# RWKV7 layer: the two inverse chains side by side, the second one's finish inside the scan, decays in place, parameters loaded early

## The chip, the cores and the metric

One core of a Trainium2 chip runs the whole program; the other cores are idle. The metric is the time of one execution in device microseconds (us). The engines are PE (matmuls), DVE (vector), ACT (activations and scaled copies), POOL (GpSimd) and SP, which here does nothing but issue DMAs: its queue is in order, so a DMA that waits for data holds every DMA behind it.

## The reference

Two transformer layers are run forward on 512 tokens of width 1024 in fp32. Layer 0 mixes with sparse attention, layer 1 with the recurrent mixer RWKV7; the change is in layer 1. What matters of it:

```
xx = shift(u) - u
proj = lambda i: (u + xx * mu[i]) @ w_in[:, part i]
r, k, v = proj(0), proj(1), proj(2)
w = -softplus(-(w0 + tanh(proj(3)) @ w_w2)) - 0.5
a = sigmoid(a0 + proj(4) @ w_a2)
kk = normalised(k * k_k);  k_mod = k * (1 + (a - 1) * k_a);  decay = exp(-exp(w))
def step(state, inp):                       # 512 steps, 16 heads of 64 x 64
    sa = einsum('bhvk,bhk->bhv', state, -kk_t)
    state = state * w_t + sa (x) (kk_t * a_t) + v_t (x) k_t
    return state, einsum('bhvk,bhk->bhv', state, r_t)
```

## The kernel before, in words

fp32 products are made of three matmuls of high and low parts; each weight tile is loaded by SP (`raw`), split by ACT (`whi`) and DVE (`wlo`). A tile framework decides the order of instructions on each engine from its own simulated times, except in the scan (`run`), whose order on PE, DVE, ACT and POOL is as written. SP's order is always the framework's.

The 512 steps are cut into 8 chunks of 64 tokens. In a chunk the recurrence is a triangular 64 x 64 system for each head, and the kernel inverts all 128 of these systems ahead of the scan, in two halves `th` of four chunks each. The stages of the layer, in order:

- `decay` and `gate` make the decay and gate projections; `decays` turns the summed decays `cums` into exponentials; `dense(1, ...)` makes the keys and hands each 128 x 512 tile to `key`, which builds the sides `A` and `B` of the systems. `root` and `normalise` scale them, `systems` multiplies and masks them and writes the systems to DRAM (`md`), `corners` and `blocks` read them back.
- `blocks(th)` inverts the 32 x 32 diagonal blocks by 31 steps of forward substitution on POOL, two dependent operations a step (L1038 and L1040, tiles `tmpi` and `two`). It is called "chain 0" and "chain 1" below.
- `whole(th)` calls `double(th)`, which joins the blocks to 64 x 64 inverses: a transposed copy (L1054, ACT), a trip through DRAM (`td`), two rounds of 128 small matmuls (L1074, L1076) and their evictions.
- Beside this, `dense(0, ...)` makes the receptances (`receive`, `bonus`) and `dense(2, ...)` the values, whose evictions (`value`) go by `tmp` to DRAM (`vpark`, L1112) and come back to `xh` by `fetch` (L1254).
- `run` is the scan: 19 cycles, two for each chunk, a cycle taking the chunk's inverse, products with the state and the output. `given(u)` (L1170) is the first product of a cycle; the second half's inverses are wanted from cycle 9 on.

The order as written ahead of the scan is chain 0 beside the receptances, `bonus`, half of the value matmuls, `whole(0)`, chain 1 beside the other half, the places of the scan, `whole(1)`, `run`.

Of the kernel before, what the change touches and what calls it, by code (L numbers as in the profile page):

```python
# [9 lines left out]
F32 = mybir.dt.float32  # L10
# [6 lines left out]
P = 128  # L17
S = 512
# [51 lines left out]
class Net:  # L70
    def __init__(self, ctx, tc, io):
        self.tc, self.nc, self.io = tc, tc.nc, io
        nc = self.nc
        self.const = ctx.enter_context(tc.tile_pool(name="const", bufs=1))
        self.act = ctx.enter_context(tc.tile_pool(name="act", bufs=1))
        self.ps = ctx.enter_context(tc.tile_pool(name="ps", bufs=4, space=PSUM))
        dram = ctx.enter_context(tc.tile_pool(name="park", bufs=1, space=bass.MemoryType.DRAM))
        self.hpark = dram.tile([S, D], F32, name="hpark")
        self.dram = dram
        self.ident = self.const.tile([P, P], F32, name="ident")  # L80
        self.mhalf = self.const.tile([P, 16], F32, name="mhalf")
# [12 lines left out]

# [330 lines left out]
    def nsa(self, xh, xl):  # L425
        nc, io = self.nc, self.io
        opair = self.open_pairs()
# [340 lines left out]
    def rwkv(self, u, layer):  # L768
# [11 lines left out]
        two = lambda: vp.tile([P, D], F32, tag="two", name="two", bufs=2)  # L780
# [6 lines left out]
        prm = vp.tile([P, 19 * KT], F32, name="prm")  # L787
        nc.sync.dma_start(out=prm[:, 0:12 * KT], in_=io["rwkv_prm"])
        mu = lambda i, kt: prm[:, i * KT + kt:i * KT + kt + 1]
        omu = lambda i, kt: mu(13 + i, kt)  # L790
        par = lambda i, j: prm[:, (6 + i) * KT + j:(6 + i) * KT + j + 1]
        W0, A0, KK, KA, RK, GB, OKA = range(7)
        for d, s, n in ((6 + OKA, 6 + KA, 1), (13, 0, 6)):
            nc.vector.tensor_scalar(prm[:, d * KT:(d + n) * KT], prm[:, s * KT:(s + n) * KT], -1.0, 1.0,
                                    op0=OP.mult, op1=OP.add)
# [4 lines left out]
        ind = vp.tile([P, KT, 32], F32, name="ind")  # L800
        nc.sync.dma_start(out=ind.rearrange("p k h -> p (k h)"), in_=self.cst("ind"))
        sel = vp.tile([64, CH], F32R, name="sel")
# [97 lines left out]
        def decays():  # L900
# [57 lines left out]
        def key(g, n, acc):  # L958

            j = 4 * g + n  # L960
            A, B = sides(j)
            if n == 0:
                n2[g] = self.bank("bon")
            sq, kk = tmp(), v3(tmp())
            nc.scalar.activation(sq, acc, AF.Square, scale=par(KK, j))
            nc.scalar.activation(kk, v3(acc), AF.Copy, scale=par(KK, j))
            nc.vector.tensor_mul(B[:, :, C:], B[:, :, C:], v3(acc))
            nc.tensor.matmul(n2[g][0:32, :], ind[:, j, :], sq, start=n == 0, stop=n == 3)
# [25 lines left out]
        rinv = [vp.tile([64, S], F32R, name="rinv", bufs=2) for _ in range(2)]  # L994
# [48 lines left out]
        def whole(th):  # L1043

            with ExitStack() as ctx:
                for i in anchor.values():
                    ctx.enter_context(self.tc.issue_after(i.ins))
                double(th)

        def double(th):  # L1050
# [14 lines left out]
            z = iv()  # L1065
            for w in range(2):
                for h, mt in enumerate(inv[th]):
# [9 lines left out]
                    for e in range(2):  # L1077
# [3 lines left out]
                        else:  # L1081
                            nc.scalar.activation(mt[r1, :, 32:64], zv[r1], AF.Copy, scale=-1.0)

# [4 lines left out]
        def bonus():  # L1088

            bon = self.bank("bon")  # L1090
            for j in range(KT):
# [3 lines left out]
                for b in range(NB):  # L1095
                    nc.tensor.matmul(bon[:, 16 * b + 2 * j:16 * b + 2 * j + 2], pr[:, b * P:b * P + P],
                                     ind[:, j, 2 * j:2 * j + 2], start=True, stop=True)
# [233 lines left out]
        weave(blocks(0), dense(0, 13, receive, vec))  # L1331
# [5 lines left out]
        weave(blocks(1), fill)  # L1337
# [8 lines left out]
        whole(1)  # L1346
# [76 lines left out]
def _consts():  # L1423
# [17 lines left out]
    parts["ind"] = ind.reshape(P, KT * 32)  # L1441
# [143 lines left out]
```

## Time and profile before

| | us |
|---|---|
| time, median of 3 runs | 2342.32 (2335.94, 2342.32, 2344.95) |
| the profiled execution: its time | 2344.54 |
| the profiled execution: its span | 2342.6 |
| PE busy | 2188.7 (93%) |
| POOL busy | 391.2 (17%) |

The span is the stretch from the first to the last recorded instruction; 1.9 us lie around it. The clock that PE was granted is 0.953 of full speed in the mean. Positions below are us from the span's start; layer 1's mixer stands between 1500 and 1930.

### The profile page before, as it was taken

The numbers are of one execution on the slowest core, as the hardware profiler recorded it, in microseconds if no ns is written. First come the engines' busy times: TensorE is split into PE (matmuls) and PEld (weight loads), VectorE is DVE, ScalarE is ACT, GpSimd is POOL, SyncE is SP. The second block draws the span as 40 slices with busy tenths as digits, with TensorE's granted clock in tenths as the row PEclk, the third lists the DMA queues.
The fourth block names the chain that finished last, engine by engine and source line by source line (L and its number), as shares of the span: only waits on it lengthen the run. The fifth ranks groups of instructions, "written<-read, shape, count | busy, mean of one in ns | idle before, by whom it ended". The sixth has DMA issues, their size and how long they took to land.

```text
span 2342.6 us, 38478 instructions
## 1 busy us (share of the span) xinstructions
PE 2188.7 (93%) x15398; PEld 1924.1 (82%) x15398; DVE 1531.3 (65%) x2446; ACT 1157.8 (49%) x2274; POOL 391.2 (17%) x397
## 2 busy tenths in 40 slices
PE   7999999999999899999999999796794988899998
PEld 7999888877656799998899998674684877899987
DVE  8888526356686888863688872486741546988733
ACT  5555415465574555553455562483332654555532
POOL 4000004031110400000310000125536433200000
PEclk9999999999899999999999999897887989999999
DMA  4333333211002233334223333223353023333332
GB/s 172 106 102 100 108 98 102 72 55 37 28 1 87 84 105 103 100 107 128 80 75 102 104 109 99 88 81 89 72 128 107 25 72 129 124 101 108 100 100 71
DMA packets 93284, 214.44 MB, mean 92 GB/s; under 512 B 40624, under 2 KB 41392, under 8 KB 93104
## 3 DMA queue, kind: packets, MB, share of 16 engines
q1 hardware_dynamic: 93104, 211.97, 29.2%
q8 instruction: 121, 1.98, 0.4%
q14 instruction: 59, 0.48, 0.1%
HBM read 196.94 MB, written 15.01 MB: 90 GB/s over the span
## 4 chain that ended last, share of the span: by engine, by line
issue 28%; PE 23%; POOL 7%; DVE 6%; ACT 2%; DMA 1%; SPq 0%; POOLq 0%; DVEq 0%; ACTq 0%
PE p L182 17%; POOL two L1040 2%; POOL tmpi L1038 2%; PE p L1146 1%; ACT junk L205 1%; POOL sp L334 1%; DVE h L248 1%; DVE slot L188 1%; DVE xl L188 0%; PE p L1191 0%; POOL rstd L209 0%; PE p L854 0%; POOL ab L915 0%; PE p L1170 0%; PE p L1162 0%
## 5 line engine op out<-in xcount | busy, mean ns | idle before, releaser
L182 PE MATMUL p<-xh,whi 128*128 128x256 f32 (+1 forms) x1640 | 479.0, 296 | 18.4 <-ACT xh L187 8.4
L182 PE MATMUL p<-xl,whi 128*128 128x256 f32 (+1 forms) x1640 | 476.9, 294 | 3.5 <-DVE xl L188 3.5
L182 PE MATMUL p<-xh,wlo 128*128 128x256 f32 (+1 forms) x1640 | 457.2, 294 | 1.5 <-DVE wlo L188 1.4
L182 PE MATMUL p<-whi,slot 128*128 128x512 f32 x1280 | 394.8, 389 | 0.0
L161 DVE TENSOR_TENSOR wlo<-raw,whi 128x1024 fp32r<-128x1024 f32 x150 | 189.9, 1268 | 313.4 <-ACT whi L157 313.3
L182 PE MATMUL p<-slot,whi 128*128 128x256 f32 x1920 | 362.1, 285 | 11.2 <-issue 6.0
L182 PEld LDWEIGHTS p<-xh,whi 128*128 128x128 f32 x1640 | 319.0, 195 | 29.6 <-ACT xh L187 9.8
L157 ACT ACTIVATE whi<-raw 128x1024 fp32r<-128x1024 f32 x166 | 174.7, 1057 | 336.8 <-PE p L182 321.0
L182 PEld LDWEIGHTS p<-xl,whi 128*128 128x128 f32 x1640 | 319.6, 195 | 9.0 <-DVE xl L188 4.9
L182 PEld LDWEIGHTS p<-slot,whi 128*128 128x128 f32 x1920 | 304.1, 193 | 13.6 <-issue 6.2
L182 PEld LDWEIGHTS p<-xh,wlo 128*128 128x128 f32 x1640 | 308.8, 195 | 7.1 <-DVE wlo L188 1.6
L187 ACT ACTIVATE whi<-xn 128x1024 fp32r<-128x1024 f32 (+1 forms) x240 | 220.0, 917 | 185.0 <-PE p L182 136.9
L188 DVE TENSOR_TENSOR wlo<-xn,whi 128x1024 fp32r<-128x1024 f32 (+1 forms) x240 | 255.3, 1065 | 50.8 <-ACT whi L187 47.6
L182 PEld LDWEIGHTS p<-whi,slot 128*128 128x128 f32 x1280 | 240.0, 188 | 49.7
L182 PE MATMUL p<-slot,wlo 128*128 128x256 f32 x960 | 270.8, 284 | 0.0
L209 POOL TENSOR_TENSOR rstd<-rstd,mhalf 128x1 f32<-128x1 f32 x48 | 30.0, 627 | 1348.5 <-DVE rstd L208 1347.6
L182 PE MATMUL p<-wlo,slot 128*128 128x512 f32 x640 | 249.0, 389 | 0.0
L182 PEld LDWEIGHTS p<-slot,wlo 128*128 128x128 f32 x960 | 185.1, 193 | 0.0
L378 ACT ACTIVATE sp<-p 128x256 f32<-128x256 f32 x320 | 121.0, 378 | 112.9 <-PE p L182 112.8
L182 PEld LDWEIGHTS p<-wlo,slot 128*128 128x128 f32 x640 | 120.1, 188 | 24.9
L188 DVE TENSOR_TENSOR wlo<-raw,whi 128x1024 fp32r<-128x1024 f32 x80 | 97.7, 1221 | 10.0 <-ACT whi L187 9.9
L187 ACT ACTIVATE whi<-raw 128x1024 fp32r<-128x1024 f32 x80 | 84.1, 1051 | 39.2 <-PE p L182 39.2
(322 smaller groups left out, 3781.6 us busy)
## 6 DMA issues: line engine op xcount, KB each, us to landing
raw<-in_wpack SPq DMA_DIRECT2D x252, 512.0 KB, 3.6
xn<-in_wpack SPq DMA_DIRECT2D x80, 512.0 KB, 3.5
hpark<-h SPq DMA_DIRECT2D x8, 512.0 KB, 2.6
h<-hpark SPq DMA_DIRECT2D x8, 512.0 KB, 4.8
h<-in_x SPq DMA_DIRECT2D x4, 512.0 KB, 7.2
gpost<-in_ffn_norm_post SPq DMA_DIRECT2D x4, 512.0 KB, 6.6
md<-tb SPq DMA_DIRECT2D x8, 256.0 KB, 3.0
td<-two SPq DMA_DIRECT2D x4, 512.0 KB, 3.0
```

What stands on the lines that cost most here:

```text
L157: self.last_hi = nc.scalar.activation(hi, raw, AF.Copy)
L161: (eng or nc.vector).tensor_sub(lo, raw, hi.bitcast(F32))
L182: m = self.nc.tensor.matmul(out, lhs[a], rhs[b], start=start and i == 0, stop=stop and i == 2, skip_group_check=more)
L187: i = self.nc.scalar.activation(hi, src, AF.Copy)
L188: return i, (eng or self.nc.vector).tensor_sub(lo, src, hi.bitcast(F32))
L205: nc.scalar.activation(self.junk(), src[q], AF.Square, scale=1.0 / (half * math.sqrt(D)), accum_out=ss[:, q:q + 1])
L209: nc.gpsimd.tensor_tensor(r[:, 1:2], r[:, 0:1], self.mhalf[:, 0:1], op=OP.pow)
L248: nc.vector.scalar_tensor_tensor(h, t[:, sl[q]], r, h, op0=OP.mult, op1=OP.add)
L334: nc.gpsimd.tensor_sub(t4, q(xh, 1, 0, b), t2)
L378: copy = lambda dst, bank: nc.scalar.activation(dst, bank[:, 0:H], AF.Copy)
L1038: nc.gpsimd.tensor_tensor(t, ms[:, j, j + 1:32].rearrange("p (i o) -> p i o", o=1).to_broadcast([P, n, m]), T[:, j:j + 1, 0:m].to_broadcas ...
L1040: nc.gpsimd.tensor_tensor(T[:, j + 1:32, 0:m], T[:, j + 1:32, 0:m], t, op=OP.subtract)
```

## The change

- **Parameters.** `prm`, the layer's mixing, decay and key parameters, was loaded and completed (L788 to L794) at the start of layer 1. Now it lies in the pool that lives all the time and `load_prm` does this at the start of layer 0.
- **Decays in place.** For each of 8 tiles, `decays` made exp into `tmp`, exp into `A`, two POOL products (L915, L917), a DVE operation and a POOL copy. Now ACT makes the second exp in place in `cums`, and an affine copy into `A`; the two POOL products are gone.
- **Keys.** `key` made two 128 x 512 ACT operations, two DVE products, a POOL product and a POOL copy (L969, L970). Now it has one large and one 128 x 8 ACT operation, three DVE operations and one POOL product (on DVE for the last tile).
- **Buffers.** `two` has four buffers, not two; `rinv` one for each, not two; `sel` lies in a `two`, `ind` is a 128 x 64 table.
- **Chains.** `blocks(1)` comes right after `blocks(0)`; chain 1 no longer runs beside the value matmuls after `whole(0)`.
- **Second inverse.** `double` is split into `convert` (transposed copy and the trip through DRAM) and two halves of matmuls. `convert(1)` is issued after cycle 5 of the scan, the halves of `double(1)` after cycles 7 and 8. Nothing of them stands ahead of the scan.

```diff
@@ -424,6 +437,7 @@
     def nsa(self, xh, xl):
         nc, io = self.nc, self.io
+        self.load_prm()
...
-        two = lambda: vp.tile([P, D], F32, tag="two", name="two", bufs=2)
+        two = lambda: vp.tile([P, D], F32, tag="two", name="two", bufs=4)
...
-                cum, aa = v3(cums[j]), B[:, :, C:]
-                em = v3(tmp())
-                nc.scalar.activation(em, cum, AF.Exp, scale=kap[:, 0:1])
-                nc.scalar.activation(A[:, :, C:], cum, AF.Exp, scale=kap[:, 1:2])
-                nc.gpsimd.tensor_mul(A[:, :, 0:C], aa, em)
-                nc.vector.tensor_scalar(aa, aa, par(KA, j), par(OKA, j), op0=OP.mult, op1=OP.add)
-                nc.gpsimd.tensor_mul(aa, aa, em)
+                nc.scalar.activation(A[:, :, C:], v3(cums[j]), AF.Exp, scale=kap[:, 1:2])
+                nc.scalar.activation(cums[j], cums[j], AF.Exp, scale=kap[:, 0:1])
+                nc.scalar.activation(A[:, :, 0:C], B[:, :, C:], AF.Identity, scale=par(KA, j), bias=par(OKA, j))
                 nc.gpsimd.tensor_copy(pc[:, j, :], A[:, :, 2 * C - 1])
...
-            sq, kk = tmp(), v3(tmp())
-            nc.scalar.activation(sq, acc, AF.Square, scale=par(KK, j))
-            nc.scalar.activation(kk, v3(acc), AF.Copy, scale=par(KK, j))
-            nc.vector.tensor_mul(B[:, :, C:], B[:, :, C:], v3(acc))
...
-            nc.gpsimd.tensor_mul(B[:, :, 0:C], kk, A[:, :, 0:C])
-            nc.gpsimd.tensor_copy(A[:, :, 0:1], kk[:, :, 0:1])
-            nc.vector.tensor_mul(A[:, :, 1:C], kk[:, :, 1:], A[:, :, C:2 * C - 1])
...
+            nc.scalar.activation(sq, acc, AF.Square, scale=kk)
+            nc.vector.tensor_mul(en, k, v3(cums[j]))
...
+            nc.vector.scalar_tensor_tensor(B[:, :, 0:C], en, kk, B[:, :, C:], op0=OP.mult, op1=OP.mult)
+            (nc.vector if j == KT - 1 else nc.gpsimd).tensor_mul(B[:, :, C:], en, A[:, :, 0:C])
+            nc.scalar.activation(A[:, :, 0:1], k[:, :, 0:1], AF.Copy, scale=kk)
+            nc.vector.scalar_tensor_tensor(A[:, :, 1:C], k[:, :, 1:], kk, A[:, :, C:2 * C - 1], op0=OP.mult, op1=OP.mult)
...
+                weave(double(th, *convert(th)))
+
+        def convert(th):
...
                 for u in range(-1, NU + 3):
                     cycle(u, X, s1, bvs, gw)
+
+                    if u == 5:
+                        dbl = double(1, *convert(1))
+                    if u >= 7:
+                        next(dbl, None)
...
-        weave(blocks(0), dense(0, 13, receive, vec))
+        weave(blocks(0))
+        weave(blocks(1))
+        weave(dense(0, 13, receive, vec))
...
         whole(0)
-        weave(blocks(1), fill)
         weave(fill)
...
         self.kinds["iv"] = (2, 3)
-        whole(1)
         run(X, *places)
```

How the order of instructions moves is seen at three places. On POOL at the end of chain 0 there stood, before, the clearing of the scan's `xh`, then the clearing of chain 1's tile and chain 1's first step:

```order
L1038 TENSOR_TENSOR tmpi<-two 128x31
L1040 TENSOR_TENSOR two<-two,tmpi 128x31
L1127 MEMSET xh 64x3072
L1032 MEMSET two 128x1024
L1033 MEMSET two 128x32
L1038 TENSOR_TENSOR tmpi<-two 128x31
L1040 TENSOR_TENSOR two<-two,tmpi 128x31
```

After the change POOL goes at the same place from the last step of chain 0 into the first steps of chain 1:

```order
L1043 TENSOR_TENSOR tmpi<-two 128x31
L1045 TENSOR_TENSOR two<-two,tmpi 128x31
L1043 TENSOR_TENSOR tmpi<-two 128x31
L1045 TENSOR_TENSOR two<-two,tmpi 128x31
L1043 TENSOR_TENSOR tmpi<-two 128x60
L1045 TENSOR_TENSOR two<-two,tmpi 128x30x2
```

The clearing of chain 1's tile has moved into chain 0, that of `xh` into chain 1, and the six L1237 products for the scan, which stood inside chain 1, behind it.

On SP, the queue ahead of the scan was before the weights, the value writes (`vpark`) with the fetches (`xh`), the reading of chain 1's systems, four weights and the other value writes:

```order
L143 DMA raw<-in_wpack 128x1024 x3
L1112 DMA vpark<-tmp 128x512 x3
L1254 DMA xh<-vpark 64x512
L1112 DMA vpark<-tmp 128x512
L1254 DMA xh<-vpark 64x512
L1030 DMA two<-md_15225 64x32x32 x2
L1254 DMA xh<-vpark 64x512
L143 DMA raw<-in_wpack 128x1024 x4
L1112 DMA vpark<-tmp 128x512 x3
```

After the change, chain 1's systems are read long before, and the writing of chain 1's result (`td_17737`) stands in this queue ahead of the value writes:

```order
L156 DMA raw<-in_wpack 128x1024 x3
L1060 DMA td_17737<-two 128x1024
L1120 DMA vpark<-tmp 128x512 x4
L1262 DMA xh<-vpark 64x512 x3
L156 DMA raw<-in_wpack 128x1024 x4
L1120 DMA vpark<-tmp 128x512 x3
```

The framework has drawn that one write of `convert(1)` ahead of the scan; the rest of it is issued in the scan. All rows behind it now wait for the end of chain 1.

On PE, before, the second inverse's matmuls stood between the first two `given` products of the scan:

```order
L1170 MATMUL p_17199<-xh,big 64x64 x7
L1074 MATMUL p_17264<-two,xl 32x32
L1074 MATMUL p_17299<-two,xl 32x32
L1074 MATMUL p_17264<-two,xl 32x32 x31
L1074 MATMUL p_17299<-two,xl 32x32 x31
L1076 MATMUL p_17334<-xl,two 32x32 x32
L1076 MATMUL p_17369<-xl,two 32x32 x32
L1162 MATMUL p_17416<-ident,ab 128x128 x4
```

After the change the next cycle's transposes follow there at once, and the first round of these matmuls is found behind cycle 7 of the scan:

```order
L1154 MATMUL p_17933<-ab 128x128
L1081 MATMUL p_17949<-two,xl 32x32 x32
L1081 MATMUL p_17984<-two,xl 32x32 x32
L1190 MATMUL p_17177<-xh,xl 64x64 x8
L1199 MATMUL p_17175<-xh,ab 64x64 x8
```

The second round stands in the same way behind cycle 8. Elsewhere, half of the decay matmuls and the gate weights' splits move ahead of the last input transposes.

## Rows read from the trace of the kernel before

**Rows 1.** Windows of 10 us at the scan's start and inside the scan.

```profile
core 0: us, PE busy (x) PEld busy (x) DVE busy (x) ACT busy (x) POOL busy (x), PEclk, DMA share, GB/s
1790.00:1800.00 10.00, 0.00 (x0) 0.00 (x0) 0.00 (x0) 0.00 (x0) 8.69 (x17) 0.50 0.00 0
...
1850.00:1860.00 10.00, 9.75 (x230) 8.61 (x228) 6.67 (x19) 6.78 (x32) 5.71 (x9) 1.00 0.10 30
```

**Rows 2.** Timeline of PE: start, length, line, and idle time before with its releaser.

```profile
1519.74 6.71 PE L854 MATMUL p<-xh,whi 128*128 128x256 f32 x16 [4.91 <-DVE whi L849]
...
1593.70 1.54 PE L968 MATMUL p<-tmp,ind 128*32 128x512 f32 x2 [1.98 <-ACT tmp L965]
...
1754.50 2.21 PE L1076 MATMUL p<-xl,two 32*32 32x32 f32 x128
...
1779.81 0.68 PE L1170 MATMUL p<-xh,big 128*64 128x64 f32 x14
1808.63 0.39 PE L1074 MATMUL p<-two,xl 32*32 32x32 f32 x4 [28.14 <-issue]
...
1820.28 0.33 PE L1170 MATMUL p<-xh,big 128*64 128x64 f32 x2 [0.78 <-DVE big L1153]
```

**Rows 3.** Timeline of POOL, chain 0 and chain 1.

```profile
1663.16 0.24 POOL L1038 TENSOR_TENSOR tmpi<-two 128x31 f32<-128x31 f32 x1 [21.08 <-DMA two<-md]
...
1719.81 0.25 POOL L1040 TENSOR_TENSOR two<-two,tmpi 128x31 f32<-128x31 f32 x1
1720.00 2.66 POOL L1127 MEMSET xh<- 64x3072 f32 x1
1756.84 0.95 POOL L1032 MEMSET two<- 128x1024 f32 x1 [34.18 <-PE p L1076]
...
1802.16 0.25 POOL L1040 TENSOR_TENSOR two<-two,tmpi 128x31 f32<-128x31 f32 x1
```

**Rows 4.** Timeline of ACT.

```profile
1517.62 1.33 ACT L829 ACTIVATE tb<-xh,prm 128x512 f32<-128x512 f32 x2 [3.01 <-DVE prm L794]
...
1592.96 0.69 ACT L965 ACTIVATE tmp<-p,prm 128x512 f32<-128x512 f32 x1 [4.62 <-POOL ab L917]
...
1612.14 1.28 ACT L977 ACT_TABLE_LOAD   x1 [0.18 <-PE p L968]
...
1802.44 1.94 ACT L1054 ACTIVATE two<-two 128x1024 f32<-128x1024 f32 x1 [25.20 <-POOL two L1040]
...
1829.02 0.77 ACT L1185 ACTIVATE xh<-p 64x256 f32<-64x256 f32 x2 [0.30 <-PE p L1182]
```

**Rows 5.** Windows by stage (columns as in rows 1).

```profile
1517.00:1566.00 49.00, 44.20 (x176) 32.72 (x177) 43.49 (x58) 40.92 (x62) 1.37 (x1) 0.91 0.31 94
1566.00:1593.00 27.00, 25.72 (x114) 20.97 (x112) 15.95 (x20) 15.33 (x23) 23.58 (x27) 1.00 0.33 110
...
1663.00:1720.00 57.00, 54.15 (x235) 45.25 (x236) 50.09 (x53) 28.25 (x39) 52.06 (x62) 0.89 0.18 54
1720.00:1764.00 44.00, 43.24 (x428) 36.56 (x427) 10.99 (x18) 14.70 (x18) 8.78 (x16) 0.92 0.75 183
1758.00:1803.00 45.00, 21.71 (x127) 17.96 (x125) 9.37 (x10) 7.22 (x10) 39.10 (x69) 0.76 0.30 94
```

**Rows 6.** Lines of ACT, 1517 to 1593: busy and mean of one, idle before.

```profile
L157 ACT ACTIVATE whi<-raw 128x1024 fp32r<-128x1024 f32 x12 | 12.4, 1051 | 4.1 <-DMA raw<-in_wpack 4.0
```

**Rows 7.** Lines of POOL, 1758 to 1803.

```profile
L1237 POOL TENSOR_TENSOR tmp<-xh,bonx 64x256 f32<-64x256 f32 x6 | 3.7, 612 | 0.4
```

**Rows 8.** Lines of DVE beside chain 0, 1663 to 1720.

```profile
L830 DVE SCALAR_TENSOR_TENSOR tb<-xh,prm,tb 128x511 f32<-128x511 f32 x16 | 15.6, 999 | 4.9 <-ACT tb L829 4.8
L832 DVE TENSOR_TENSOR big<-tb,big 128x512 fp32r<-128x512 f32 x15 | 14.7, 1000 | 0.0
```

**Rows 9.** Timeline of SP's queue ahead of the scan.

```profile
1772.61 1.68 SPq L1112 DMA_DIRECT2D vpark<-tmp  x3
1777.08 1.89 SPq L1254 DMA_DIRECT2D xh<-vpark  x3
```

**Rows 10.** The page's DMA issues: KB each, us from issue to landing.

```profile
raw<-in_wpack SPq DMA_DIRECT2D x252, 512.0 KB, 3.6
```

More of the change, by code (lines that the diff above doesn't have):

```diff
@@ L83, in __init__ @@
         self.wpool = ctx.enter_context(tc.tile_pool(name="wpool", bufs=1))
+        self.prm = self.const.tile([P, 19 * KT], F32, name="prm")
         self.chunk = 0
@@ L93, in cst, with prm_parts, load_prm @@
         return self.io["consts"][0:rows, c0:c0 + n]
+    def prm_parts(self):
+        mu = lambda i, kt: self.prm[:, i * KT + kt:i * KT + kt + 1]
+        return mu, lambda i, kt: mu(13 + i, kt), lambda i, j: mu(6 + i, j)
+    def load_prm(self):
+        self.nc.sync.dma_start(out=self.prm[:, 0:12 * KT], in_=self.io["rwkv_prm"])
+        for d, s, n in ((12, 9, 1), (13, 0, 6)):
+            self.nc.vector.tensor_scalar(self.prm[:, d * KT:(d + n) * KT], self.prm[:, s * KT:(s + n) * KT], -1.0, 1.0,
+                                         op0=OP.mult, op1=OP.add)
     def push(self, name, **kw):
@@ L785, in rwkv @@
         self.junk = lambda: vp.tile([P, 512], F32, tag="tb", name="junk", bufs=2)
[L787 to L791, printed above, removed]
+        prm, (mu, omu, par) = self.prm, self.prm_parts()
         W0, A0, KK, KA, RK, GB, OKA = range(7)
-        for d, s, n in ((6 + OKA, 6 + KA, 1), (13, 0, 6)):
-            nc.vector.tensor_scalar(prm[:, d * KT:(d + n) * KT], prm[:, s * KT:(s + n) * KT], -1.0, 1.0,
-                                    op0=OP.mult, op1=OP.add)
         own = [slice(0, 64), slice(64, 128)]
@@ L799, in rwkv @@
         nc.sync.dma_start(out=tri, in_=self.cst("tri"))
-        ind = vp.tile([P, KT, 32], F32, name="ind")
-        nc.sync.dma_start(out=ind.rearrange("p k h -> p (k h)"), in_=self.cst("ind"))
-        sel = vp.tile([64, CH], F32R, name="sel")
+        ind = vp.tile([P, 64], F32, name="ind")
+        nc.sync.dma_start(out=ind, in_=self.cst("ind"))
+        sel = two().bitcast(F32R)[0:64]
         st = big()
@@ L963, in key @@
                 n2[g] = self.bank("bon")
-            sq, kk = tmp(), v3(tmp())
-            nc.scalar.activation(sq, acc, AF.Square, scale=par(KK, j))
-            nc.scalar.activation(kk, v3(acc), AF.Copy, scale=par(KK, j))
-            nc.vector.tensor_mul(B[:, :, C:], B[:, :, C:], v3(acc))
-            nc.tensor.matmul(n2[g][0:32, :], ind[:, j, :], sq, start=n == 0, stop=n == 3)
-            nc.gpsimd.tensor_mul(B[:, :, 0:C], kk, A[:, :, 0:C])
-            nc.gpsimd.tensor_copy(A[:, :, 0:1], kk[:, :, 0:1])
-            nc.vector.tensor_mul(A[:, :, 1:C], kk[:, :, 1:], A[:, :, C:2 * C - 1])
+            k, kk = v3(acc), par(KK, j)
+            sq, en = tmp(), v3(tmp())
+            nc.scalar.activation(sq, acc, AF.Square, scale=kk)
+            nc.vector.tensor_mul(en, k, v3(cums[j]))
+            nc.tensor.matmul(n2[g][0:32, :], ind[:, 30 - 2 * j:62 - 2 * j], sq, start=n == 0, stop=n == 3)
+            nc.vector.scalar_tensor_tensor(B[:, :, 0:C], en, kk, B[:, :, C:], op0=OP.mult, op1=OP.mult)
+            (nc.vector if j == KT - 1 else nc.gpsimd).tensor_mul(B[:, :, C:], en, A[:, :, 0:C])
+            nc.scalar.activation(A[:, :, 0:1], k[:, :, 0:1], AF.Copy, scale=kk)
+            nc.vector.scalar_tensor_tensor(A[:, :, 1:C], k[:, :, 1:], kk, A[:, :, C:2 * C - 1], op0=OP.mult, op1=OP.mult)
         def root(g, ts=slice(0, S)):
@@ L993, in rwkv @@
         md = [self.dram.tile([32, 2, C, C], F32, name=f"md{th}") for th in range(2)]
-        rinv = [vp.tile([64, S], F32R, name="rinv", bufs=2) for _ in range(2)]
+        rinv = [vp.tile([64, S], F32R, name="rinv", bufs=1) for _ in range(2)]
         def systems(g, th):
@@ L1064, in double @@
                         nc.sync.dma_start(out=mt[r0:r0 + 32, :, 32 * k:32 * k + 32], in_=tv[0, k, e, :, hq[h], :])
-            z = iv()
+            return t11, iv()
+        def double(th, t11, z):
             for w in range(2):
@@ L1082, in double @@
                             nc.scalar.activation(mt[r1, :, 32:64], zv[r1], AF.Copy, scale=-1.0)
+                yield
         def receive(g, n, acc):
@@ L1096, in bonus @@
                     nc.tensor.matmul(bon[:, 16 * b + 2 * j:16 * b + 2 * j + 2], pr[:, b * P:b * P + P],
-                                     ind[:, j, 2 * j:2 * j + 2], start=True, stop=True)
+                                     ind[:, 30:32], start=True, stop=True)
                 yield
@@ L1440, in _consts @@
     ind = (h == 2 * p + (i // 64)[:, :, None]).astype(f)
-    parts["ind"] = ind.reshape(P, KT * 32)
+    parts["ind"] = (np.arange(64)[None, :] == 30 + i // 64).astype(f)
     sel = np.zeros((P, KT, P), f)
```

2 lines of the change are left out of this document (removed).

## The prediction

> **What bounds the kernel now.** I read the 10 us windows around the scan's start first. From 1790 to 1800 PE, DVE and ACT do nothing at all and only POOL works; inside the scan PE is busy 9.75 of 10 us [rows 1]. So the scan is bound by PE, and ahead of it stands a hole in which everything waits for POOL. PE's timeline shows its edges: the first `given` ends at 1780.5, the second inverse's matmuls start at 1808.6, the second `given` comes at 1820.3 [rows 2]. POOL's timeline says why: chain 0 runs from 1663.2 to 1720.0, then POOL stands idle for 34 us until the first inverse's matmuls have given a buffer free, and chain 1 runs from 1757.8 to 1802.4 [rows 3]. ACT's transposed copy follows at once after 25 us of waiting [rows 4]. That is the path: keys, systems, chain 0, (idle,) chain 1, join, scan. Chain 0's own start waits for `md`, so what lies upstream of it counts too: there ACT waits 4.6 us for POOL's `ab` products before the first key eviction at 1592.96 [rows 4], and POOL is busy 23.6 of 27 us [rows 5].
>
> **A. Upstream of chain 0: about 13 us.** What holds the first key eviction? PE's first matmul with its key tile follows at 1593.70 after 1.98 us without work, so PE had done all it could by 1591.7 [rows 2]. 48 matmuls of the second key group stand between the first group's end and that point; at 25.72 us for 114 matmuls [rows 5] these are 10.9 us, so the first group was ready at 1580.8, and the eviction was late by ACT and POOL. After the change, POOL's 16 products are gone and ACT has a row of its own work. ACT was busy 40.92 + 15.33 = 56.3 us between 1517 and 1593 [rows 5]. Three weight splits of 1.05 us go ahead of that stretch [rows 6], eight affine copies come in at the 0.69 us of the 128 x 512 eviction [rows 4]: 56.3 - 3.2 + 5.5 = 58.6. I add 5 us of stalls (it had 19.7, of them 4.6 for POOL's product and 3.0 for `prm` [rows 4]) and start at 1516.8: 1580.4, which is 12.6 earlier. PE can follow: it drops 13 of its 32 first decay matmuls and the 4.9 us wait for `whi` [rows 2]. From this eviction to `root` were 19.2 us [rows 4]; the waits for `tmp` shorten it by about 2, DVE's third operation per tile gives back 1 to 2. I take 13 in all. Bounds: 4 if PE's clock falls in the gaps that it then gets, as it did to 0.50 where it starved [rows 1], or DVE becomes the limit; 20 if the stalls vanish and the second group gains as well.
>
> **B. The hole: about 30 us.** I count in the frame in which chain 0 still starts at 1663.2. Chain 0 is 56.9 us long, chain 1 44.6 with six L1237 products of 3.7 us and their gaps of 0.4 [rows 3, 7], so 40.4 by itself. Why is chain 0 longer for the same 62 operations? It runs beside 50.1 us of DVE work, chain 1 beside 9.4; POOL is busy 52.1 and 39.1 - 3.7 = 35.4 us [rows 5]. The slope is (52.1 - 35.4) / (50.1 - 9.4) = 0.41 us for each us of DVE. Chain 1 moves next to the stretch from 1720 to 1764, where DVE is busy 11.0 [rows 5]: 40.4 + 0.7 = 41.1. Its clearing (0.95, with a small one 1.1) and that of `xh` (2.7) [rows 3] now lie inside the chains. The end: 1663.2 + 56.9 + 1.1 + 41.1 + 2.7 = 1765.0.
>
> This is ahead of the first `given` (1779.8 to 1780.5), and the scan no longer waits for the second inverse there. Without that wait the second `given` follows the first by 1.1 us of transposes, 2.1 of products and 0.8 of mask: 1784.4 and not 1820.3 [rows 2], so 35.9 us go. But the write of chain 1's result now stands in SP's queue ahead of the value writes, and SP passes it only at 1765.0. Behind it: this write and four value writes at 1.68/3 = 0.56, 2.8; three fetches, 1.9 [rows 9]; a weight, 0.5 to issue and 3.6 to land [rows 10]; its split on ACT, 1.05 [rows 6], which stands ahead of the second value group's evictions; then the first eviction, 0.7. That is 1775.6, and the first write of that group at about 1776.5 to 1777, as DVE's evictions have a split ahead of them as well, where it was 1772.6 [rows 9]: 4.5 late. It costs between nothing (if the path is elsewhere) and 15 (if the evictions wait for three more weights at 3.6 each). PE then starves for some us at the lower clock: 1. So 35.9 - 4.5 - 1 = 30.4.
>
> **C. What the scan takes on: about 7 us.** The two halves of the second `double` now stand in PE's order: 2.21 us each [rows 2], and a little for ACT's evictions ahead of the next cycle's, 2.4 and 2.5. The transposed copy, 1.94 [rows 4], stands in ACT's order, where PE's product and ACT's next operation are 0.30 us apart [rows 4]: 1.7. Small waits add 0.4. The sum is 7.0; it could be 4.7 (the matmuls alone, if ACT has the room), or 17 if cycle 9 also has to wait for the trip through DRAM, which before lay in the 6.2 us between 1802.4 and 1808.6 [rows 2, 4].
>
> **D. Parameters at the start: nothing.** One load and two tiny DVE operations move to the program's start, behind the first loads of the input; no row here shows that place. If nothing covers them they cost SP 0.56 for the issue [rows 9] and DVE less than twice the 0.69 of a 128 x 512 operation, 2 us together; if DVE still waits for the input there, nothing. They are nearer to that, having 8 and 48 elements a partition against 512. Their other effect, ACT's 3.0 us wait, is in A.
>
> **The sum** against the profiled execution: 13 + 30.4 - 7 = 36.4, so 2344.5 - 36.4 = 2308.1. The median of the runs shown is 2.2 us below the profiled execution: 2306.
>
> **A rule on POOL and DVE.** The rows say that DVE's work lengthens chain 0 by 0.41 us for each us [rows 5]. Of DVE's 50.1 us there, 30.3 are operations with two inputs in SBUF, L830 and L832 [rows 8]. [...]
>
> **The rivals.**
> 1. *Chain 1 slow beside other work* (0.12). If it takes chain 0's 56.9 us instead of 41.1, its end is 1780.8, SP is held 15.8 longer: 2306 + 16 = 2322. For it: it moves next to work of PE, ACT and DMA. Against: that work is PE's, DVE is nearly idle there [rows 5].
> 2. *The hold is not felt and upstream gives 20* (0.10): 4.5 + 1 + 7 more, with 2 more from C: 2306 - 14.5 = 2291. For it: 19.7 us of ACT idle; against: PE is busy 69.9 of 76 us there [rows 5].
> 3. *Upstream gives nothing* (0.12). The freed POOL is not what decides, DVE's third operation or PE's half clock takes it: A falls to 0 to 4, 2306 + 11 = 2317.
> 4. *The second inverse is late in the scan* (0.07): cycle 9 waits up to 10 us, 2316. For it: the trip was 6.2 us and more. Against: from cycle 5 to cycle 7 there are two full cycles for it.
> 5. *The write at SP decides* (0.03), the slower side: chain 1's end holds the value path, and so the whole start of the scan, which before it did not. The gains are gone when SP is held until about 1765 + 36 = 1801, and it is slower by 0.5% from 1813: chain 1 would have to take 89 us, 2354 and more. The longest chain seen took 56.9.
>
> **How the numbers follow.** The likeliest case has 0.56, its own range being 2296 to 2316 by the bounds of A and B. The range 2286 to 2327 takes in rivals 1 to 4 at their price and leaves out two of them together and rival 5. A measurement tells about 0.5% from no change: 2330.6 and 2354 are the borders. All of the main case and rival 2, and most of 1, 3 and 4 lie below: faster 0.90; pairs of rivals reach no change: 0.07; slower 0.03.
>
> **What would show it.** Right: POOL's idle row of 34 us is gone, chain 1's first step follows chain 0's last at once and takes about 41 us; chain 0 starts near 1650; the windows without PE are gone, the second `given` comes 3 to 5 us after the first; the first key eviction is near 1580; two cycles of the scan are longer by 2.4 us, one by 1.7, and no PE wait at cycle 9. Wrong: chain 0 starts within 4 us of 1663, or chain 1 takes over 50 us, or SP's write of `td` ends a wait that reaches the scan's first products by more than 10 us.

## The result and the profile after

The changed kernel takes 2304.68 us (median of 4 runs, 2298.61 to 2306.79), the kernel before 2343.64 beside it: a ratio of 0.9833, 95% interval 0.98 to 0.9866. It is 39 us faster by the medians and 38.1 by the two profiled executions (2344.54 and 2306.49, the latter with a span of 2304.6); forecast were 36.4, and a median of 2306.

POOL's timeline after the change answers to [rows 3]:

```profile
1647.88 0.24 POOL L1043 TENSOR_TENSOR tmpi<-two 128x31 f32<-128x31 f32 x1 [22.45 <-DMA two<-md]
...
1704.42 0.25 POOL L1045 TENSOR_TENSOR two<-two,tmpi 128x31 f32<-128x31 f32 x1
1704.75 0.24 POOL L1043 TENSOR_TENSOR tmpi<-two 128x31 f32<-128x31 f32 x1
...
1720.55 2.66 POOL L1135 MEMSET xh<- 64x3072 f32 x1
...
1748.77 0.25 POOL L1045 TENSOR_TENSOR two<-two,tmpi 128x31 f32<-128x31 f32 x1
```

The idle row of 34 us is gone. Chain 0 starts at 1647.9 and chain 1's first step follows chain 0's last at once; chain 0 takes 56.8 us, chain 1 44.3 with the 2.7 of clearing `xh`, so 41.6 by itself. PE's timeline answers to [rows 2] (L1178 is `given`, L1154 `products`, L1081 and L1083 are the second inverse's matmuls):

```profile
1762.46 1.71 PE L1154 MATMUL p<-ab 64*128 64x128 f32 x16 [2.22 <-DVE tmp L1117]
...
1769.20 1.11 PE L1178 MATMUL p<-xh,big 128*64 128x64 f32 x14
...
1774.15 1.71 PE L1178 MATMUL p<-xh,big 128*64 128x64 f32 x16 [0.78 <-DVE big L1161]
...
1815.91 2.21 PE L1081 MATMUL p<-two,xl 32*32 32x32 f32 x128
...
1823.95 2.21 PE L1083 MATMUL p<-xl,two 32*32 32x32 f32 x128
```

Between the first `given` and the second there are 4 us, where there were 40, and the second inverse's matmuls stand in the scan. But PE still waits 2.22 us for DVE's eviction ahead of 1762.46, and runs slower for a while: the 16 matmuls of the second `given` take 1.71 us, where 14 took 0.68 in [rows 2]. The 10 us windows show it (columns as in [rows 1], the granted clock third from the end):

```profile
1750.00:1760.00 10.00, 10.00 (x47) 8.03 (x45) 0.95 (x1) 0.51 (x1) 0.00 (x0) 1.00 0.91 320
1760.00:1770.00 10.00, 7.78 (x55) 6.58 (x52) 6.14 (x8) 3.69 (x6) 1.23 (x2) 0.73 0.67 208
1770.00:1780.00 10.00, 8.32 (x76) 6.69 (x74) 2.58 (x4) 2.13 (x5) 2.45 (x4) 0.59 0.35 99
1780.00:1790.00 10.00, 9.59 (x222) 8.53 (x224) 4.38 (x11) 5.82 (x25) 2.27 (x3) 1.00 0.10 29
```

The clock is 0.73 and 0.59 of full speed between 1760 and 1780, behind the gap. SP's queue tells why there is a gap; it answers to [rows 9]:

```profile
1749.06 0.33 SPq L1060 DMA_DIRECT2D td<-two  x1
1749.47 2.57 SPq L1120 DMA_DIRECT2D vpark<-tmp  x4
1752.46 1.75 SPq L1262 DMA_DIRECT2D xh<-vpark  x3
1754.31 7.85 SPq L156 DMA_DIRECT2D raw<-in_wpack  x4
1762.26 1.40 SPq L1120 DMA_DIRECT2D vpark<-tmp  x3
```

The write of chain 1's result leaves when chain 1 ends, and the value writes, the fetches, four weights and the second group's value writes follow it one behind the other. This stretch, in which SP's queue stands behind that write, is called the hold. ACT's rows show how it reaches PE: the split of a weight waits 9.79 us for its load, and the second value group's evictions stand behind the split, though the matmuls that they wait for end at 1759.8:

```profile
1759.49 1.06 ACT L170 ACTIVATE whi<-raw 128x1024 fp32r<-128x1024 f32 x1 [9.79 <-DMA raw<-in_wpack]
1760.57 1.08 ACT L1119 ACTIVATE tmp<-p 128x512 f32<-128x512 f32 x2
```

ACT's timeline answers to the first key eviction in [rows 4] (1592.96 there, behind 4.62 us of waiting that are gone):

```profile
1578.01 0.67 ACT L970 ACTIVATE tmp<-p,prm 128x512 f32<-128x512 f32 x1
```

**By stages.** The stretch ahead of the mixer, where no edit touches more than the parameters' load, differs by up to 13 us from one profile to the next (below). So all profiles are read from the mixer's first transposes of the input (the first matmul with `ident` and `xn` behind 1490 us; 1500.88 in the kernel before, 1499.75 after). Each figure in the table is the start of that row, for "ends" its end, less that zero; the last column is the span less it.

| kernel | first key eviction | chain 0 starts | chain 1 ends | value matmuls end | second `given` | scan, first to last inverse product | end |
|---|---|---|---|---|---|---|---|
| before | 92.1 | 162.3 | 301.5 | 273.1 | 319.4 | 76.6 | 841.7 |
| changed | 78.3 | 148.1 | 249.3 | 260.1 | 274.4 | 83.8 | 804.9 |
| e1, chains alone | 84.5 | 152.9 | 254.9 | 264.8 | 284.3 | 83.5 | 815.0 |
| e2, upstream alone | 78.5 | 148.8 | 288.3 | 260.4 | 307.6 | 76.2 | 829.7 |
| e3, write behind fetches | 78.6 | 149.5 | 250.5 | 261.3 | 269.9 | 83.1 | 798.2 |
| e4, load called late | 78.6 | 149.0 | 250.2 | 261.1 | 275.9 | 83.2 | 805.5 |
| e5, joined before scan | 78.5 | 148.9 | 249.0 | 273.6 | 286.4 | 76.0 | 805.3 |
| e6, half of chain 1 | 78.5 | 148.8 | 229.7 | 260.7 | 269.3 | 83.2 | 797.9 |
| e7, tile's pool alone | 84.5 | 152.7 | 292.6 | 264.6 | 310.2 | 76.4 | 832.1 |
| e8, tile in layer's pool | 84.5 | 155.6 | 258.5 | 266.9 | 285.1 | 85.2 | 812.8 |
| c1, changed again | 78.5 | 149.1 | 250.2 | 261.0 | 275.9 | 83.3 | 804.8 |
| c2, e3 again | 78.5 | 149.0 | 249.9 | 260.7 | 269.3 | 83.5 | 797.9 |
| e9, join eased | 78.4 | 149.4 | 249.7 | 273.9 | 282.5 | 80.5 | 808.2 |
| e10, one input | 78.5 | 149.6 | 246.2 | 261.9 | 271.6 | 84.1 | 801.8 |

One order of instructions, profiled three times (changed, c1, e4), has 804.9, 804.8 and 805.5 in the last column, and differs by up to 1.5 us in between. So a difference of 2 us in the last column is readable, where single runs of one kernel spread by 8 to 13.

### The profile page after: what moved, and what is told of

It is laid out like the page before. It is cut to its first block, busy times and chain, and to the rows that moved or that the text cites. A ratio compares the mean times of both kernels' runs of the same rounds, so it can differ in the third digit from the quotient of the medians.

```text
span 2304.6 us, 38449 instructions
## 1 busy us (share of the span) xinstructions
PE 2190.6 (95%) x15398; PEld 1921.0 (83%) x15398; DVE 1527.2 (66%) x2447; ACT 1159.3 (50%) x2282; POOL 363.9 (16%) x372
## 4 chain that ended last, share of the span: by engine, by line
issue 29%; PE 24%; DVE 5%; POOL 4%; ACT 3%; DMA 1%; SPq 0%; DVEq 0%; POOLq 0%; ACTq 0%
PE p L195 19%; POOL two L1045 1%; POOL tmpi L1043 1%; PE p L1154 1%; ACT junk L218 1%; POOL sp L347 1%; PE p L1178 0%; DVE slot L201 0%; PE p L1170 0%; DVE xl L201 0%; DVE h L261 0%; PE p L972 0%; PE p L862 0%; PE p L1206 0%; PE p L1199 0%
## 5 line engine op out<-in xcount | busy, mean ns | idle before, releaser
L174 DVE TENSOR_TENSOR wlo<-raw,whi 128x1024 fp32r<-128x1024 f32 x150 | 190.2, 1269 | 316.7 <-ACT whi L170 316.7
L195 PEld LDWEIGHTS p<-slot,whi 128*128 128x128 f32 x1920 | 303.4, 193 | 14.9 <-issue 6.2
L195 PE MATMUL p<-wlo,slot 128*128 128x512 f32 x640 | 249.0, 389 | 0.0
L195 PE MATMUL p<-big,whi 128*128 128x512 f32 (+1 forms) x288 | 94.9, 412 | 12.0 <-ACT big L839 11.2
L200 ACT ACTIVATE whi<-raw 128x1024 fp32r<-128x1024 f32 x80 | 84.1, 1051 | 40.1 <-PE p L195 40.1
```

Of the source, the lines that this page charges most:

```text
L174: (eng or nc.vector).tensor_sub(lo, raw, hi.bitcast(F32))
L195: m = self.nc.tensor.matmul(out, lhs[a], rhs[b], start=start and i == 0, stop=stop and i == 2, skip_group_check=more)
L200: i = self.nc.scalar.activation(hi, src, AF.Copy)
```

## The experiments

**The parts taken apart (e1, e2).** e1 has the new chains with decays, keys and the call that loads the parameters as they were; e2 is the reverse.

```diff
 e1
-        self.load_prm()                        # at the start of layer 0
+        self.load_prm()                        # at the start of layer 1
-  (the new bodies of decays and key)
+  (the bodies of before)
 e2
-        weave(blocks(0))
-        weave(blocks(1))
-        weave(dense(0, 13, receive, vec))
+        weave(blocks(0), dense(0, 13, receive, vec))
...
         whole(0)
+        weave(blocks(1), fill)
         weave(fill)
...
+        whole(1)
         run(X, *places)
```

> The changed kernel with decays and key made as before and the parameters loaded at the start of layer 1; only the chains, the second inverse in the scan and the buffers are changed. Theory (the terms add up): chain 0 starts again near 1663 us, the second given comes about 31 us earlier than in the kernel before, the scan is 7 longer: 24 us faster than before, about 2320. Rival (the moved chains are the whole gain): about 2305, with chain 0 starting near 1648. Rival (without the earlier start the moved chains give nothing): about 2343.

Measured: 2312.01 us, ratio 0.9875 (0.9849 to 0.99).

> The changed kernel with the chains, the second inverse, the two-buffer tile and sel as before; decays, keys and the early parameters stay. Theory: chain 0 starts near 1648 us, everything behind it keeps its old distances, hole included: 15 us faster than before, about 2328. Rival (the earlier start is lost in the waits behind it): 2343.

Measured: 2334.1 us, ratio 0.9967 (0.9951 to 0.9982).

Neither came out as expected. e1 gained 29 us and not 24, and its table row says where: its first key eviction and chain 0 come 7.6 and 9.4 us earlier than before although its decays and keys are the old ones. Something upstream was still in it. e2 gained 7 by the median and 12 by the table: chain 0 is 13.5 earlier, as forecast, but the second `given` only 11.8. PE's row between the two rounds of the second inverse shows a wait for SP's read that the kernel before does not have:

```profile
1802.54 3.62 PE L1083 MATMUL p<-xl,two 32*32 32x32 f32 x126 [1.29 <-DMA xl<-td]
```

The clock has dropped in the hole, as before (0.64 from 1760 to 1800), but now the second `given` itself and the products behind it run at the lower level (0.50 from 1800 to 1810, 0.74 from 1810 to 1820, by e2's windows; in the kernel before it was back at 1.00 from 1820, with the second `given`). The two gains, 36 by the medians, come near to that of the change, but this proves nothing: the next runs show that one part is counted in both.

**What of the parameters it was (e4, e7, e8).** e4 moves only the call `load_prm` back to the start of layer 1.

```diff
 e4
-        self.load_prm()                        # in nsa, layer 0
+        self.load_prm()                        # ahead of prm_parts, layer 1
 e7, on the kernel before
+        self.prm = self.const.tile([P, 19 * KT], F32, name="prm")   # beside ident and mhalf
-        prm = vp.tile([P, 19 * KT], F32, name="prm")
+        prm = self.prm
 e8, on the changed kernel
-        self.prm = self.const.tile([P, 19 * KT], F32, name="prm")
+        self.prm = vp.tile([P, 19 * KT], F32, name="prm")           # and load_prm behind it
```

> The changed kernel with one thing undone: the parameters are loaded at the start of layer 1. Theory: they are the smaller part of what lies upstream of chain 0, the 3 us wait on ACT and the 3 weight splits of 1.05 us behind it: about 6 us slower than the changed kernel, 2311, chain 0 near 1654. Rival (ACT's own row of work decides, the parameters do nothing): 2305. Rival (the parameters are all of it, the decays and keys nothing): 2320, chain 0 near 1662.

Measured: 2308.85 us, ratio 0.9856 (0.9828 to 0.9883); chain 0 at 149.0 in the table. Every engine has the same instructions in the same order as in the changed kernel: the call's place in the program does nothing. SP issues the load at 6.75 us in e4 and at 6.87 in the changed kernel: the framework draws it to the program's start either way, where its tile is free. So e4 undid nothing, and e1 had the early parameters too. The place that counts is the tile's pool:

> The kernel before with one thing changed: the parameters' tile lies in the pool that lives all the time; all else, the chains too, is as before. Theory of the prediction (ACT's and POOL's work on decays and keys holds the first key eviction, the parameters are worth 3 to 6 us): 2338 to 2341. Rival, from the first four runs (the layer's pool holds the load back and with it the decay matmuls; this is most of the earlier start): chain 0 starts 9 us earlier against the mixer's first transposes, and the time is 9 us less, 2334.

Measured: 2329.02 us, ratio 0.9953 (0.9932 to 0.9973); 9.6 us less in the table.

> The changed kernel with the parameters' tile back in the layer's own pool. Theory of the prediction: 3 to 6 us slower than the changed kernel, chain 0 about 151 to 154 us after the mixer's first transposes. Rival (the tile's place is most of the earlier start): 9 us slower, 2314, chain 0 about 157 us after them.

Measured: 2307.63 us, ratio 0.9858 (0.9834 to 0.9882); 7.9 us more than the changed kernel in the table.

By the table both come near to the rival (9 us in each), and the prediction's price of 3 to 6 is too low. The medians say less: e7 is 12.6 us faster than the kernel before, but e8 only 3.0 slower than the changed kernel's first runs, which would fit the price; its profile reaches the mixer at 1493.03, 6.7 us ahead of the changed kernel's. Its chain 0 starts at 155.6, between the 151 to 154 of the theory and the rival's 157. The mechanism stands in the rows of e8: SP's load, DVE's completion and first use of the parameters, and PE's first decay matmuls:

```profile
1507.49 0.33 SPq L101 DMA_DIRECT2D prm<-in_rwkv_prm  x1
```

```profile
1509.54 0.26 DVE L104 TENSOR_SCALAR prm<-prm 128x8 f32<-128x8 f32 x2 [1.38 <-DMA prm<-in_rwkv_prm]
...
1510.92 1.89 DVE L857 TENSOR_TENSOR whi<-raw,prm 128x512 f32<-128x512 f32 x3
```

```profile
1512.36 5.24 PE L862 MATMUL p<-xh,whi 128*128 128x256 f32 x16 [4.93 <-DVE whi L857]
```

The tile in the layer's pool is not there before the layer begins, and the load is issued at 1507.5, 14 us behind the mixer's first transposes; the two completions and the weights' products follow, and PE waits 4.93 us for them. In e7, with the tile in the other pool and all else as before, the same matmuls start 5.3 us after those transposes and not 19:

```profile
1497.33 5.41 PE L855 MATMUL p<-xh,whi 128*128 128x256 f32 x16 [2.41 <-ACT xh L764]
```

**What SP's queue holds back (e3, c1, c2, e6).** e3 puts the one write of chain 1's result behind the first six fetches; e6 leaves out the last 15 of chain 1's 31 steps, so that the second half's inverses are not complete.

```diff
 e3
-            nc.sync.dma_start(out=td[1], in_=T.rearrange("p i k -> p (i k)"))
+            with ExitStack() as ctx:
+                if th:
+                    ctx.enter_context(self.tc.issue_after(fetched[NX - 1].ins))
+                nc.sync.dma_start(out=td[1], in_=T.rearrange("p i k -> p (i k)"))
 e6
-            for j in range(31):
+            for j in range(31 - 15 * th):
```

> The changed kernel with the write of chain 1's result (the one DMA that stands ahead of the value writes) put behind the first six fetches in SP's queue. Theory as in the prediction (the hold costs 4.5 us and a stretch at the lower clock): the value writes of the second group go about 4.5 us earlier after the value matmuls, the first given comes 2 to 3 us after their end and not 7; 4 to 6 us faster than the changed kernel. Rival (PE ends the value matmuls 10.8 us after chain 1's end anyway, and only the last evictions are held): 1 to 2 us. Rival (nothing of it is felt): 0.

Measured: 2292.86 us, ratio 0.9797 (0.9776 to 0.9818).

> The changed kernel with the last 15 of chain 1's 31 steps left out, so chain 1 ends some 15 to 20 us earlier; the second half's inverses are not complete. It asks what the chains still bound. Rival (the POOL chain is still the path, as it was before): 12 us faster or more than the changed kernel. Theory (PE with its value matmuls has taken over, chain 1 is felt by SP's queue alone): the value matmuls end where they did, the time falls by what the hold costs, 1 to 6 us.

Measured: 2292.8 us, ratio 0.9801 (0.9777 to 0.9825).

The two are the same, though chain 1 ends at 250.5 in e3 and 229.7 in e6. So POOL's chain is no longer the path; only the write that waits for it is. (The 12 us of e6 alone would have fitted its rival; beside e3's 12 they do not.) But that both gain 12 us by the medians is twice what was expected, and the table gives 7. To tell, the changed kernel and e3 ran again beside each other:

> The changed kernel itself once more, beside the others of this call, since the stretch ahead of the mixer (which no edit touches) differed by up to 13 us between profiles. Every theory: within 0.3% of 2305 as against the kernel before; from the mixer's first transposes to the end of the span 805 us, as in its first profile.

Measured: 2309.15 us, ratio 0.9867 (0.9843 to 0.9892).

> The changed kernel with the write of chain 1's result behind the first six fetches, once more. Theory (the hold costs what the stages show, 6 us): 6 us faster than the changed kernel of this call, and 798 to 799 us from the mixer's first transposes to the end. Rival (the 12 us between the medians of two calls are all its own): 12 us faster than the changed kernel of this call.

Measured: 2298.53 us, ratio 0.9812 (0.9785 to 0.9839); the table has 6.9.

Of the hold, 6.7 and 6.9 us are shown stage by stage in two pairs of profiles (804.9 and 804.8 against 798.2 and 797.9). Between the medians of c1 and c2 lie 10.6, nearer to the rival's 12. What the medians add can hardly be the edit's: in e3 and c2 every engine has the changed kernel's instructions in the changed kernel's order, but for nine places in SP's queue from 1749 us on. It is as large as the spread ahead of the mixer, where no place differs; that it comes from there is not shown run by run. c1's PE rows show where the 6.9 lie; its value matmuls end at 1753.15:

```profile
1768.00 0.33 PE L1178 MATMUL p<-xh,big 128*64 128x64 f32 x2 [0.78 <-DVE big L1161]
1768.60 0.68 PE L1178 MATMUL p<-xh,big 128*64 128x64 f32 x14 [0.27 <-DVE big L1161]
...
1770.88 0.68 PE L1190 MATMUL p<-xh,xl 64*64 64x64 f32 x16
```

From there to the second `given` are 14.9 us, in c2 8.6 (1757.42 to 1765.99). In c2 the same weight is split on ACT, without a wait for its load, 5.6 us before the value matmuls end, and the evictions follow the matmuls at once:

```profile
1751.86 1.06 ACT L170 ACTIVATE whi<-raw 128x1024 fp32r<-128x1024 f32 x1 [4.54 <-PE p L195]
```

It is by this that e3 is the best complete version of the study, at 0.98 of the kernel before.

**The second inverse's place (e5, e9).** e5 finishes it ahead of the scan, as before, with the chains back to back. e9 has e3's write, and issues the rest of `convert(1)` ahead of the scan, with half of the scan's evictions on DVE.

```diff
 e5
-                    if u == 5:
-                        dbl = double(1, *convert(1))
-                    if u >= 7:
-                        next(dbl, None)
...
+        whole(1)
         run(X, *places)
 e9, on e3
-                    if u == 5:
-                        dbl = double(1, *convert(1))
+            dbl = double(1, *convert(1))       # ahead of the scan
...
-                            nc.scalar.activation(z[r2, hq[h], :], zv[r2], AF.Copy)
+                            if th and e:
+                                nc.vector.tensor_copy(z[r2, hq[h], :], zv[r2])
+                            else:
+                                nc.scalar.activation(z[r2, hq[h], :], zv[r2], AF.Copy)
```

> The changed kernel with the second inverse finished ahead of the scan; the chains stay back to back. Theory (back to back is what empties the hole; the place of the second inverse is worth little): the scan loses its 7 us, the start of the scan takes on 4 to 7 us of matmuls at the lower clock and about 6 us of reads in SP's queue ahead of the value writes: about 4 us slower than the changed kernel, 2308. Rival (the move into the scan is what brings it): the scan's start waits 18 us from the end of chain 1, as it did before, and the time is 2315 or more.

Measured: 2308.04 us, ratio 0.986 (0.9838 to 0.9882); the table has 805.3, the same as the changed kernel.

> The changed kernel with the write behind the fetches and, beside that, the rest of the second inverse's conversion ahead of the scan (its ACT copy in the idle time behind the value evictions) and half of the scan's evictions of the second inverse on DVE. Theory (what the scan takes on is ACT's time next to 4.4 us of matmuls): the cycle that took the copy falls from 6.58 to 5.12 us, the two with the matmuls by 0.4 to 1 each; 2 to 3 us faster than with the write moved alone. Rival (the evictions are hidden, only the matmuls count): 1.5. Rival (DVE's share delays the state's update instead): no gain or a loss.

Measured: 2304.41 us, ratio 0.9845 (0.982 to 0.9869); the table has 10.2 us more than c2.

e5's time fits (3.4 us slower by the medians, about 4 expected), its reason doesn't: the value matmuls end 13.6 us later than in the changed kernel, which neither theory said, and the scan is 7.8 shorter. e9 has the same, and is slower than c2, by the medians 5.9, where 2 to 3 us faster was expected. ACT's timeline of e9 shows why (L1059 is the transposed copy of chain 1's result, L1090 an eviction of the *first* inverse):

```profile
1749.53 1.94 ACT L1059 ACTIVATE two<-two 128x1024 f32<-128x1024 f32 x1 [12.97 <-POOL two L1045]
1751.48 1.19 ACT L1090 ACTIVATE two<-p 32x512 f32<-32x512 f32 x2
```

The framework has put the copy, which waits 13 us for the end of chain 1, ahead of the first inverse's other evictions; these hold half of PE's second round, and that the value matmuls, as PE's row shows:

```profile
1752.72 1.92 PE L1083 MATMUL p<-xl,two 32*32 32x32 f32 x64 [10.20 <-ACT two L1090]
```

In the changed kernel the copy stands in cycle 6 of the scan's order, and can't come early. So here the scan's order is worth more as a fence, which keeps the copy from coming early, than as a place to hide the matmuls. e9's own theory did hold in the scan, which is 3.0 us shorter than c2's (80.5 against 83.5; 2 to 3 were expected), but it was paid for ahead of it. A kernel with e3's write, the copy left in the scan and half the evictions on DVE was not run.

**What lengthens chain 0 (e10).** The low parts of the receptances' and values' inputs are a copy of one tile, no difference of two, so these products lack their correction.

```diff
-            eng.tensor_sub(l, x, h.bitcast(F32))
+            if i in (0, 2):
+                eng.tensor_scalar(l, x, 0.0, None, op0=OP.mult)
+            else:
+                eng.tensor_sub(l, x, h.bitcast(F32))
```

> The changed kernel with the low parts of the receptances' and values' inputs taken as a copy with one input instead of a difference of two tiles (so these products lack their correction). It asks what lengthens chain 0. Theory (operations of DVE with two inputs in SBUF and POOL's reads take turns): 16 of the 40 or so such operations beside chain 0 are gone, chain 0 falls from 56.5 us by about 5, to 51 or 52. Rival (DVE's being busy as such): chain 0 stays at 55 to 57.

Measured: 2300.74 us (one run). Chain 0 takes 52.7 us from its first step to its last; in c1 56.9. The lines of DVE around it (busy us and mean ns behind the bar), first c1's, then e10's:

```profile
L838 DVE SCALAR_TENSOR_TENSOR tb<-xh,prm,tb 128x511 f32<-128x511 f32 x16 | 15.1, 973 | 5.5 <-ACT tb L837 5.4
L840 DVE TENSOR_TENSOR big<-tb,big 128x512 fp32r<-128x512 f32 x16 | 15.1, 962 | 3.8 <-ACT big L839 3.7
```

```profile
L838 DVE SCALAR_TENSOR_TENSOR tb<-xh,prm,tb 128x511 f32<-128x511 f32 x16 | 15.4, 968 | 7.6 <-ACT tb L837 7.5
...
L841 DVE TENSOR_SCALAR big<-tb 128x512 fp32r<-128x512 f32 x16 | 10.4, 647 | 0.5 <-PE p L195 0.2
```

The 16 operations cost DVE 4.7 us less, and chain 0 is 4.1 shorter. The slope of 0.41 would have given 1.9. So the theory's 5 was near, and the rival's 55 to 57 is out. The edit makes DVE's operations shorter as well as giving them one input, but POOL's rows tell the two apart. Each POOL operation is held against the shortest of its line and size: beside L840 alone (two inputs in SBUF) it takes 0.27 us longer in the mean (5 cases in c1), beside the one-input L841 alone 0.07 (2 in e10), and beside L1094, one of whose inputs lies in PSUM, 0.00 (3 in c1). The cases are few, but it is the form with two inputs in SBUF that costs here. Where few operations overlap, the changed kernel's own trace shows single meetings. First DVE's rows, then POOL's around them, at the start and at the end of chain 1:

```profile
1707.30 0.69 DVE L840 TENSOR_TENSOR big<-tb,big 128x512 fp32r<-128x512 f32 x1 [3.44 <-ACT big L839]
...
1744.64 1.42 DVE L174 TENSOR_TENSOR wlo<-raw,whi 128x1024 fp32r<-128x1024 f32 x1 [9.47 <-ACT whi L170]
```

```profile
1707.03 0.37 POOL L1043 TENSOR_TENSOR tmpi<-two 128x112 f32<-128x112 f32 x1
1707.48 0.79 POOL L1045 TENSOR_TENSOR two<-two,tmpi 128x112 f32<-128x112 f32 x1
...
1710.04 0.46 POOL L1043 TENSOR_TENSOR tmpi<-two 128x156 f32<-128x156 f32 x1
...
1745.05 1.24 POOL L1043 TENSOR_TENSOR tmpi<-two 128x112 f32<-128x112 f32 x1
1746.37 0.43 POOL L1045 TENSOR_TENSOR two<-two,tmpi 128x112 f32<-128x112 f32 x1
```

DVE's operation comes first and takes its 0.69 us; POOL's, which starts 0.18 us later, takes 0.79, where the same operation takes 0.43 at 1746.37. At the end DVE's split of a weight comes first, and POOL's takes 1.24 where the same takes 0.37 at 1707.03. Beside chain 0 it also goes the other way: c1's L840 takes 962 ns in the mean, against the 0.69 us here. So POOL's operations are 0.36 and 0.87 us longer in these two meetings, where DVE's came first; what decides in general which of the two is lengthened, and by how much, no run here shows. The slope of 0.41 is then a mean over operations that meet and don't, and need not hold for another mix.

## Why the prediction was right, point by point

**A, upstream, forecast 13.** Chain 0 starts 15.3 us earlier, of which 1.1 are ahead of the mixer, so 14.1. The first key eviction is 13.8 earlier in the table, forecast 12.6. The reason held too, that ACT's own row of work sets this eviction: the forecast had 58.6 us of work and 5 of stalls from 1516.8 in the frame of the kernel before, and after the change ACT is busy 58.55 of the 62.5 us ahead of it (columns as in [rows 1]):

```profile
1515.50:1578.00 62.50, 55.46 (x220) 40.97 (x220) 43.79 (x62) 58.55 (x89) 2.58 (x9) 0.95 0.23 71
```

What the two halves are worth by themselves was not weighed right: of these 13.8 us, the tile's pool alone brings 7.6 (e7), the decays and keys alone 7.6 (e8). The prediction gave the parameters the 0.8 and 3.2 us on ACT and found the rest in the 5 us of stalls that it left; that the load itself was late because of its tile's pool, and with it the decay matmuls, it did not see. (PE has 32 decay matmuls fewer in this stretch, not 13.)

**B, the hole, forecast 30.4.** The second `given` is 45.0 earlier in the table, less the 14.1 of A 30.9. Step by step: chain 0 at 56.8 (56.9), chain 1 at 41.6 (41.1 by the slope of 0.41), the end of chain 1 at 1749.0, which in the prediction's frame (plus the 15.3) is 1764.3 (1765.0). The hold, 4.5 and 1 at the clock, was the guess with the widest bounds, 0 to 15. It came about as forecast, by the weight, its split on ACT and the evictions behind it; moving the write behind the fetches gives 6.9, so it was taken 1.4 too small. The lower clock (0.59 from 1770 to 1780) is felt behind the second `given`: from there to the first inverse product are 4.4 us, where there were 2.9.

**C, the scan, forecast 7.0.** The scan is 83.8 - 76.6 = 7.2 longer. ACT's rows are the three that are new:

```profile
1804.50 2.02 ACT L1059 ACTIVATE two<-two 128x1024 f32<-128x1024 f32 x1
...
1817.15 2.39 ACT L1087 ACTIVATE two<-p 32x512 f32<-32x512 f32 x4 [0.81 <-PE p L1081]
...
1825.20 2.41 ACT L1089 ACTIVATE xl<-p 32x512 f32<-32x512 f32 x4 [0.81 <-PE p L1083]
```

The cycle with the copy takes 6.6 us and not 5.1; the two with the matmuls and the one behind them 7.3, 8.0 and 5.9 (starts of the inverse product at 1804.21, 1810.79, 1818.05, 1826.09 and 1832.01): 1.5, 2.2, 2.9 and 0.8 more. Forecast were 1.7 once and 2.4 twice, and small waits. ACT's four evictions of 2.4 us hold the next cycle's first eviction, so the two halves cost more than their 2.21 us on PE.

**The rivals.** Chain 1 slow beside other work: no, 41.6. The hold not felt and upstream 20: no, 6.9 and 14.1. Upstream nothing: no. The second inverse late: no, cycle 9's inverse product (1826.09) starts with the end of the matmuls ahead of it. The write at SP decides: it is felt, at 6.9 us, far from the 36 that would have eaten the gain.

**D**, the start: no cost that the rows show (SP issues the load in 0.43 us at 6.87, DVE's two operations take 0.25 at 20.57); the first transposes are 1.1 us earlier, inside their spread.

What the change is made of, by the ends in the table: the tile's pool 9.6 (before to e7), on top of it the chains 17.1 (e7 to e1), on top of both the decays and keys 10.1 (e1 to changed). These shares hold for this order of the parts: without the moved chains the decays and keys bring 2.4 (e7 to e2). With them they bring more than the 4.8 by which chain 0 comes forward, since the hold is longer without them: from the value matmuls' end to the second `given` pass 19.5 us in e1, 18.2 in e8, 14.3 in the changed kernel. In e1 the write of chain 1's result stands one weight further ahead in SP's queue; in e8 it stands where it does in the changed kernel, but chain 1 ends 8.4 us ahead of the value matmuls' end, there 10.8. How much each of the two brings, no run here shows.

## What to carry to other kernels

A tile that is loaded once and used late belongs in a pool that is free when the load could go (9.6 us in e7); where a scheduler orders the instructions, ask for the tile's lifetime: moving the call alone changed no instruction's place here. A wait on a queue was paid here by what stood behind it, on ACT's queue (in e9 the copy waited 13.0 us, and PE 10.2 for an eviction behind it) as on SP's (6.9 us, c1 against c2): look where the scheduler puts the operation that waits for the slowest chain. And read differences from a point just ahead of the change; the median of whole runs here can't tell 7 us from 12.

## What was not expected of the hardware

The same instructions in the same order (changed, e4, c1) reach the mixer at 1499.75, 1504.72 and 1492.12 us. Nearly all of it arises between 390 and 777 us, in layer 0's attention: at 389 us the three are within 1.5 us, at 777 the second is 4.8 behind the first and the third 7.7 ahead. The windows from 600 to 700 us of the three, in that order:

```profile
600.00:700.00 100.00, 98.65 (x406) 64.66 (x405) 75.39 (x209) 61.33 (x162) 13.84 (x9) 0.86 0.04 11
```

```profile
600.00:700.00 100.00, 98.45 (x411) 65.89 (x411) 72.97 (x200) 59.43 (x157) 14.77 (x10) 0.85 0.04 11
```

```profile
600.00:700.00 100.00, 98.63 (x430) 63.08 (x428) 80.93 (x225) 68.26 (x180) 13.85 (x9) 0.93 0.04 11
```

PE was granted 0.86, 0.85 and 0.93 of full speed there, and did 406, 411 and 430 matmuls. In the first of the three, of the fifty windows of 2 us in this stretch 35 are at 1.00, 11 at 0.50 and 4 in between. Why one execution is granted more than the next, no run here shows; the 12.6 us between the second and the third are as large as many an edit's effect.
